# A runtime check for overfull experts moved from unit 10 to unit 3, with its transfers on POOL's queue

## The chip, the cores and the metric

The kernel runs on one core of a Trainium2 chip. A core has five engines with a queue each: TensorE (PE; its weight loads are shown apart as PEld), VectorE (DVE), ScalarE (ACT), GpSimd (POOL) and SyncE (SP), which in this kernel issues the DMA transfers. All transfers are carried by the same 16 DMA engines. The metric is the device time of one execution in microseconds (us).

## The reference

One layer of a decoder for 512 tokens of width 1024 in float32. After a mixing part (gated convolution, block-sparse attention, output projection, layer norm) comes a mixture of experts: each token picks one of 4 groups and in it 2 of 8 experts, so 2 of 32. Expert `e` computes the following on its tokens, and its result is added to the token's row with a weight:

```python
hid = jax.nn.silu(xb @ w_gate[e]) * (xb @ w_up[e])
return hid @ w_down[e]
```

A gated per-layer embedding is added, and a last layer norm closes the layer. How many tokens an expert gets is known only at run time.

## The kernel before

**Units.** The 32 experts are sorted by their number of tokens and cut into 12 units, `KINDS = "PPPQPQPQPQPP"`: a P unit holds 2 experts with 64 places each, a Q unit 4 experts with 32 places each. Unit 3 is the first Q unit, unit 4 a P unit, unit 10 the last but one. The loop over `n` runs them in order. A unit has 8 steps `gate_up` (a slice of 128 input channels each, PE rows `L1003`), a `swiglu`, and 4 steps `down` (`L1023`), for which `f` counts from 0 to 3. Between the steps PE does other work that is due (`pace`, `fill`): it gathers the tokens of later units (`L764`, `L765`), adds the results of the last unit to the tokens' rows (`scatter`, `L1035`), and works on the per-layer embedding. `drain` does what is left of it. Unit 11 has down steps of its own (`last_down`, `L1340`), and after them come the last scatters (`L1352`, `L1353`), the layer norm and the stores.

**Loads.** 24 slots of 1 MB lie in on-chip memory. Each step of a P unit needs one slot of weights and each step of a Q unit two; a slot is filled by two transfers of 512 KB that SP issues (`L266`; `L273` for the last four). `pump` hands out slots to the loads in the order of the queue for as long as more than `reserve` slots are free; `serve` calls it after each step with 0. A transfer that fills a used slot waits on SP for the last reader of the slot, and SP issues in order, so everything behind it waits too. At most eight transfers are under way. Where `queue[0][0]` stands in `closed`, the pump stops: the constants of the last norm (`("ln2",)`, issued at `L235`) are held back in this way until unit 11.

**The check.** An expert with more tokens than places needs further passes. `count_blocks` in unit 2 writes the number of these passes to `nxi`. `overflow` loads that number on each engine (`L1066`) and jumps over the body where it is zero (`L1067`); on the inputs timed here it is zero. Every engine runs this code. The arm that is taken for zero passes adds to each engine's semaphore, and to that of each transfer queue used in the body, what the body would have added. An engine or queue first waits there for its own earlier work. The body borrows the first four free slots. Before the change, `overflow` stands in unit 10, between its last `down` and the copies out of its result (`L1029`, `L1030`).

Of the kernel before, what the change touches and what calls it, by code (L numbers as in the profile page):

```python
# [18 lines left out]
P = 128  # L19
# [13 lines left out]
NU = len(KINDS)  # L33
NFIX = 4
# [17 lines left out]
PLE = {5: 5, 6: 1, 7: 4, 8: 1, 9: 5}  # L52
WEIGHTS = {"P": [1.5, 0, 1.5, 0] + [5, 2.5] + [0, 1, 0], "Q": [2, 2, 2, 1.5] + [3, 2] + [1, 2, 1]}
LAST = [4, 0, 4, 0, 2, 2]


C_ID = 0
# [7 lines left out]
C_KEY = C_MASK + P  # L65
C_KE = C_KEY + (NBLK - 1) * NE
C_KO = C_KE + (NBLK - 1) * NE
C_END = C_KO + (NBLK - 1) * NE
# [31 lines left out]
def hybrid_moe_layer_kernel(ctx: ExitStack, tc: tile.TileContext, xT, xtok, pT, w_in, w_conv, w_out, ln1, w_r,  # L100
                            b_r, w_e, w_last, w_pg, w_pp, ln2, cst, out):
    nc = tc.nc
# [5 lines left out]
    slots = Slots(upool, N_SLOTS)  # L108
    banks = {"mm": 2, "s": 3, "y": 2, "z": 1}

    def ps(tag):
        return psum.tile([P, 512], F32, tag=tag, name=f"ps_{tag}", bufs=banks[tag])

    def sm(name, shape, dtype=F32, bufs=2):
        return spool.tile(list(shape), dtype, tag=name, name=name, bufs=bufs)
# [20 lines left out]

    queue = deque()
    loaded = {}
    closed = {("ln2",), ("e", NFIX // 2, 0, 0)}

    def pump(reserve, ahead=99):
        while queue and slots.left() > reserve and len(loaded) < ahead and queue[0][0] not in closed:
            key, src, shape = queue.popleft()
            b = slots.take(shape)
            if callable(src):
                src(b.t)
            else:
                nc.sync.dma_start(b.t, src)
            loaded[key] = b

    wants, got = deque(), {}

    def claim(key, shape, dtype=F32, urgent=False):

        (wants.appendleft if urgent else wants.append)((key, shape, dtype))

    def serve(all_=True):
        while wants and slots.left():
            key, shape, dtype = wants.popleft()
            got[key] = slots.take(shape, dtype)  # L160
        if all_ and not wants:
            pump(0)

    def grab(key):
        if key not in got:
# [3 lines left out]
    def need(key):  # L169
        while key not in loaded:  # L170
            pump(slots.left() - 1)
        return loaded.pop(key)
# [76 lines left out]
    for n in sorted(PLE):  # L249
        t = sum(len(v) for v in tasks.values())  # L250
        tasks[n] = list(range(t, t + PLE[n]))
    rows_of, base = w_e.rearrange("n u p i d -> (n u p i) d"), {}
# [490 lines left out]
    def ple_start():  # L743

        for j in range(2):
            for i in range(2):
                claim((("x", j), i), [P, KD, 2 * P], F32R)
            yield (("x", j), 1)
            ple["x", j] = [grab((("x", j), i)) for i in range(2)]
            add(3.6, ple_turn(j))  # L750
            yield
# [18 lines left out]
    def ple_chunk(c):  # L770
        for i in range(2):
            claim((("pg", c), i), [P, KD, 256], F32R)
        yield (("pg", c), 1)
        yield from halve(("pg", c), need(("pg", c)))
# [244 lines left out]
    def down(o, f, ht, ws, cap):  # L1019
        for h in range(2):  # L1020
            for i, w in enumerate(ws):
                r = slice(i * cap, (i + 1) * cap)
                nc.tensor.matmul(o[h][r], ht[:, f, r], w[:, h * 512:(h + 1) * 512], start=(f == 0), stop=(f == 3))  # L1023
# [41 lines left out]
    def overflow():  # L1065
        nv = nc.values_load(nxi[0:1, 0:1], min_val=0, max_val=2 * T // CAP + NE)  # L1066
        with tc.If(nv > 0):  # L1067
            own = list(slots.q)
            ws, wb, tb, kb = own[0:4]
            kt = upool.tile([P, 4 * T], F32, tag=f"u{kb}", name="kt")  # L1070
            n = (NBLK - 1) * NE
            nc.sync.dma_start(kt[:, 0:3 * n], cst[:, C_KEY:C_END])
            kv, ke, ko, keys = (kt[:, i * n:(i + 1) * n].rearrange("p (b e) -> p b e", e=NE) for i in range(4))
            find_blocks(keys)
            nc.vector.tensor_mul(keys, keys, kv)
# [7 lines left out]
            with tc.For_i(0, nv) as _:  # L1083
# [18 lines left out]
                rv = nc.values_load(ei[0:1, 0:1], min_val=0, max_val=(NP - 1) * ROWS + 1)  # L1102
# [23 lines left out]
                def piece_of(u):  # L1126
                    t = upool.tile([P, 2, D], F32, tag=f"u{ws}", name="wo")
                    for r in range(2):
                        nc.sync.dma_start(t[:, r], rows_of[bass.ds(rv + (2 * u + r) * 2 * P, P, 2)])
                    return t  # L1130

                o = [ps("mm") for _ in range(2)]
                for u in range(4):
                    t = piece_of(u)
# [6 lines left out]
                for u in range(2):  # L1141
                    t = piece_of(4 + u)
# [10 lines left out]
    def add(cost, gen, lane=1):  # L1153
        lanes[lane].append((cost, gen))
# [22 lines left out]
    def fill(share):  # L1177

        spare[0] += share * (rest(0) + rest(1))
        while (lanes[0] or lanes[1]) and spare[0] > 0:  # L1180
            spare[0] -= any_piece()
        spare[0] = min(spare[0], 1.0)
# [7 lines left out]
    def chore():  # L1190

        while chores and (lack[0] is None or lack[0] in got):
            try:
                lack[0] = next(chores[0])
                return True
            except StopIteration:
                chores.popleft()
        return False
# [3 lines left out]
    def place_pair(n):  # L1202
        places[n] = t = sm("pt", [P, T], F32R, bufs=1)
        e, m, cap = UNITS[n]
        place(t, lambda tt: rmb[:, tt, e:e + m], m, cap)
        yield 0.3
# [13 lines left out]
    for n in range(NU):  # L1220
        g, r = GROUP_OF[n]
        ne, cap = UNITS[n][1:]
        o = [ps("mm") for _ in range(2)]
        point = [0]

        def pace():
            w = (LAST if n == NU - 1 else WEIGHTS[KINDS[n]])[point[0]:]
            if w[0]:
                fill(w[0] / sum(w))
            point[0] += 1  # L1230

        def pieces(u):
            return [need(("e", n, j, u)) for j in range(ne // 2)]

        if scat is not None:
            add(3.6, scat, 0)
        add(0.3, place_pair(n), 0)
        done[:] = [0.0, 0.0]
        ahead = n == GROUPS[g][-1] and g + 1 < NG
        if ahead:  # L1240
            claim(("xe", g + 1), [P, KD, GROUP], F32, True)
            if g % 2:
                claim(("pts", g + 1), [P, NT, 2 * GROUP], F32R, True)
        for t in tasks.get(n, []):
            add(3.5, ple_task(t))
        if n + 2 == min(tasks):
            chores.append(ple_start())
        for t in tasks.get(n + 1, []):
            if t % NT == 0:
                chores.append(ple_chunk(t // NT))  # L1250
        chore()
        for k in range(KD):
            bs = pieces(k)
            gate_up(o, k, [xe[g].t[:, k, r * P + i * cap:r * P + (i + 1) * cap] for i in range(ne)],
                    [b.t[:, i] for b in bs for i in range(2)])
            slots.give(*bs)
            if n == NU - 1 and k == 1:
                closed.clear()
                slots.q.rotate(-4)
            serve()  # L1260
            if k == 1 and ahead:
                select(g + 1)
                add(7.7 if len(GROUPS[g + 1]) > 1 else 5.3, gather_group(g + 1))
            if k > 0:
                chore()
            if n == 0 and k == 0:
                next(weights)
                next(steps)
            if n == 0 and k == 1:
                rank(mc, 0, NT, NE)  # L1270
                next(weights)
            if n == 0 and k == 4:
                late[0] = group_weights(0)
                next(late[0])
            if r == 0 and k == 6:
                for _ in late.pop(g):
                    pass
            if n == 2 and k == 6:
                count_blocks()
            if k % 2:  # L1280
                pace()
        h = sm("hw", [P, FE], bufs=1)
        swiglu(h, o, wsl[g][r], P)
        pace()
        ht = turn_hidden(h, P)
        pace()
        if n == NU - 1:
            drain()
            break
        o = [ps("y") for _ in range(2)]  # L1290
        if n == 0:
            for j in range(2):
                claim(("acc", j), [P, 2, D])
        for f in range(4):
            bs = pieces(8 + f)
            down(o, f, ht, [b.t[:, i] for b in bs for i in range(2)], cap)
            slots.give(*bs)
            if f == 3:
                claim("y", [P, 4 * T], F32R, True)
            serve()  # L1300
            chore()
            if f < 3:
                pace()
        y = grab("y")
        if n == NU - 2:
            overflow()
            serve()
        for h in range(2):
            split_out(halves(y.t, h), o[h], P)
        scat = scatter_pair(n, y.t, y)  # L1310
        while chore():
            pass
        if n == NU - 2:
            drain()
        if n == GROUPS[g][-1]:
            drain()
            slots.give(xe.pop(g))

    n, y, sq, diag = NU - 1, slots.take([P, 4 * T], F32R), slots.take([P, 512]), slots.take([P, 2, P])
    pt = places.pop(n)  # L1320
# [2 lines left out]
    u = sm("u", [P, 2, NT], bufs=1)  # L1323
# [227 lines left out]
```

## Time and profile before

| what | value |
|---|---|
| median of 3 runs | 764.24 us (761.93 to 764.78) |
| the profiled execution | 761.77 us, of it 760.0 us span from the first to the last instruction |
| PE busy | 727.2 us, 96% of the span |
| DMA | 233.52 MB, 307 GB/s over the span |
| mean granted TensorE clock | 0.994 of full speed |

The span is shown in the profile in 40 slices of 19 us. Times "at 704.3" below are us from the span's start. An engine's idle time is put down to what ended it; a busy PE is not PE at its peak, since matmuls overlap and their ends are modelled.

### The profile page before, as it was taken

The numbers are of one execution on the slowest core, as the hardware profiler recorded it, in microseconds if no ns is written. First come the engines' busy times: TensorE is split into PE (matmuls) and PEld (weight loads), VectorE is DVE, ScalarE is ACT, GpSimd is POOL, SyncE is SP. The second block draws the span as 40 slices with busy tenths as digits, with TensorE's granted clock in tenths as the row PEclk, the third lists the DMA queues.
The fourth block names the chain that finished last, engine by engine and source line by source line (L and its number), as shares of the span: only waits on it lengthen the run. The fifth ranks groups of instructions, "written<-read, shape, count | busy, mean of one in ns | idle before, by whom it ended". The sixth has DMA issues, their size and how long they took to land. (4 is left out here: it accounts for less than half of the span.)

```text
span 760.0 us, 11561 instructions
## 1 busy us (share of the span) xinstructions
PE 727.2 (96%) x4338; PEld 431.2 (57%) x4338; DVE 312.5 (41%) x657; ACT 163.9 (22%) x340; POOL 66.5 (9%) x93
## 2 busy tenths in 40 slices
PE   7999999999999899999989999999999999999896
PEld 4787887787878336335723437444465444653243
DVE  4656544647588426251525103332023321223246
ACT  5445544243021101010312001200012000110015
POOL 0215335100000000000000000000000000100002
PEclk9999999999999999999999999999999999999999
DMA  8500401355509999999999999999999999999972
GB/s 297 225 1 1 166 1 35 132 229 223 213 5 374 421 411 362 376 410 409 406 410 408 391 401 356 374 408 409 403 406 394 409 410 408 409 407 410 407 261 111
DMA packets 61979, 233.52 MB, mean 307 GB/s; under 512 B 6864, under 2 KB 10592, under 8 KB 56032
## 3 DMA queue, kind: packets, MB, share of 16 engines
q1 hardware_dynamic: 61920, 232.75, 78.2%
q8 instruction: 35, 0.57, 0.3%
q14 instruction: 24, 0.20, 0.1%
HBM read 230.62 MB, written 2.10 MB: 306 GB/s over the span
## 5 line engine op out<-in xcount | busy, mean ns | idle before, releaser
L1003 PE MATMUL ps_mm<-big,big 128*64 128x512 f32 (+1 forms) x1024 | 217.1, 603 | 12.8 <-DMA big<-in_w_e_dram 9.4
L1003 PEld LDWEIGHTS ps_mm<-big,big 128*64 128x64 f32 (+1 forms) x1024 | 56.2, 123 | 148.4 <-issue 87.9
L1044 DVE TENSOR_TENSOR big<-big,ps_s 128x512 f32<-128x512 f32 x80 | 52.0, 683 | 129.3 <-PE ps_s L1035 129.3
L132 PE MATMUL ps_mm<-big,big 128*128 128x512 f32 (+1 forms) x240 | 89.9, 375 | 3.4 <-ACT big L118 3.4
L133 PE MATMUL ps_mm<-big,big 128*128 128x512 f32 (+1 forms) x240 | 87.1, 363 | 0.2 <-DVE big L119 0.2
L134 PE MATMUL ps_mm<-big,big 128*128 128x512 f32 (+1 forms) x240 | 86.9, 362 | 0.1
L1023 PE MATMUL ps_y<-big,ht 128*32 128x512 f32 (+1 forms) x480 | 82.9, 604 | 0.7 <-ACT ht L1016 0.7
L119 DVE TENSOR_TENSOR big<-big,big 128x512 fp32r<-128x512 f32 (+1 forms) x74 | 58.5, 823 | 27.5 <-ACT big L118 26.9
L118 ACT CAST big<-big 128x512 fp32r<-128x512 f32 (+1 forms) x74 | 50.6, 727 | 43.3 <-DVE big L433 20.1
L1035 PE MATMUL ps_s<-big,pt 128*128 128x512 f32 x176 | 57.9, 433 | 0.7 <-DVE big L1044 0.6
L132 PEld LDWEIGHTS ps_mm<-big,big 128*128 128x128 f32 x240 | 45.3, 189 | 14.3 <-ACT big L118 4.8
L134 PEld LDWEIGHTS ps_mm<-big,big 128*128 128x128 f32 x240 | 45.3, 189 | 7.8 <-DVE big L119 0.6
L133 PEld LDWEIGHTS ps_mm<-big,big 128*128 128x128 f32 x240 | 45.3, 189 | 6.7 <-DVE big L119 0.8
L1035 PEld LDWEIGHTS ps_s<-big,pt 128*128 128x128 f32 x176 | 28.5, 189 | 32.6 <-issue 24.7
L807 POOL TENSOR_TENSOR big<-big,ps 128x256 f32<-128x256 f32 x16 | 11.8, 735 | 400.6 <-issue 178.1
L375 POOL TENSOR_SCALAR big<-big,rden 128x128 f32<-128x128 f32 (+3 forms) x32 | 39.1, 1232 | 70.5 <-DVE rden L373 70.5
L1023 PEld LDWEIGHTS ps_y<-big,ht 128*32 128x32 f32 (+1 forms) x480 | 22.0, 124 | 40.7 <-issue 37.1
L813 PEld LDWEIGHTS ps_s<-big,big 128*128 128x128 f32 x320 | 41.4, 190 | 5.9 <-issue 3.3
L813 PE MATMUL ps_s<-big,big 128*128 128x256 f32 x320 | 43.8, 285 | 0.1
L132 PE MATMUL ps_s<-big,big 128*128 128x256 f32 x128 | 37.0, 289 | 0.1
L134 PE MATMUL ps_s<-big,big 128*128 128x256 f32 x128 | 36.2, 283 | 0.0
L133 PE MATMUL ps_s<-big,big 128*128 128x256 f32 x128 | 36.2, 283 | 0.0
(263 smaller groups left out, 765.0 us busy)
## 6 DMA issues: line engine op xcount, KB each, us to landing
big<-in_w_e_dram SPq DMA_DIRECT2D x336, 512.0 KB, 10.1
big<-in_w_e_dram SPq DMA_DIRECT2D x24, 1024.0 KB, 15.2
big<-in_w_in_dram SPq DMA_DIRECT2D x11, 1024.0 KB, 6.4
big<-in_w_out_dram SPq DMA_DIRECT2D x4, 1024.0 KB, 5.9
big<-in_w_pg_dram SPq DMA_DIRECT2D x4, 1024.0 KB, 9.3
big<-in_xtok_dram SPq DMA_DIRECT2D x2, 1024.0 KB, 6.9
out_dram<-big SPq DMA_DIRECT2D x8, 256.0 KB, 2.0
big<-in_xT_dram SPq DMA_DIRECT2D x3, 512.0 KB, 8.5
```

The lines of the kernel that those rows point to most:

```text
L118: nc.scalar.copy(hi, raw)
L119: nc.vector.tensor_sub(lo, raw, hi.bitcast(F32))
L132: nc.tensor.matmul(o, ah, bh, start=first, stop=False)
L133: nc.tensor.matmul(o, ah, bl, start=False, stop=False)
L134: nc.tensor.matmul(o, al, bh, start=False, stop=last)
L375: nc.gpsimd.tensor_scalar(pr[h][:, 0:ks], pr[h][:, 0:ks], rden[:, h:h + 1], None, op0=ALU.mult)
L807: nc.gpsimd.tensor_tensor(r, r, s, op=ALU.add)
L813: nc.tensor.matmul(o[:, 0:n], src[tt // 2].t[:, tt % 2, k * P:(k + 1) * P], pt(tt), start=(i == 0), stop=(i == 2 * NT - 1))
L1003: nc.tensor.matmul(o[a][i * m:(i + 1) * m], x, w[:, a * FE:(a + 1) * FE], start=(k == 0), stop=(k == KD - 1))
L1023: nc.tensor.matmul(o[h][r], ht[:, f, r], w[:, h * 512:(h + 1) * 512], start=(f == 0), stop=(f == 3))
L1035: nc.tensor.matmul(o, pt[0:m, tt * P:(tt + 1) * P], y[i][0:m], start=(i == 0), stop=(i == 1))
L1044: nc.vector.tensor_add(r, r, o)
```

## The change

The check is made at the end of unit 3 (`CHECK = 3`), after the unit's result is copied out and all work due is drained. For the last two down steps of that unit the pump keeps four slots back (`kept[0] = 4`) and gives them out after the check. The transfers inside the body are issued by POOL (`nc.gpsimd`) in place of SP. The constants of the last norm are no longer held back, and the four slots at the end are no longer set apart (`slots.q.rotate(-4)` goes).

```diff
+CHECK = 3
-    closed = {("ln2",), ("e", NFIX // 2, 0, 0)}
+    closed = {("e", NFIX // 2, 0, 0)}
-    wants, got = deque(), {}
+    wants, got, kept = deque(), {}, [0]
...
         if all_ and not wants:
-            pump(0)
+            pump(kept[0])
...
-            nc.sync.dma_start(kt[:, 0:3 * n], cst[:, C_KEY:C_END])
+            nc.gpsimd.dma_start(kt[:, 0:3 * n], cst[:, C_KEY:C_END])
...
-                        nc.sync.dma_start(t[:, r], rows_of[bass.ds(rv + (2 * u + r) * 2 * P, P, 2)])
+                        nc.gpsimd.dma_start(t[:, r], rows_of[bass.ds(rv + (2 * u + r) * 2 * P, P, 2)])
...
-            if n == NU - 1 and k == 1:
-                closed.clear()
-                slots.q.rotate(-4)
...
             bs = pieces(8 + f)
+            kept[0] = 4 if n == CHECK and f > 1 else 0
...
-        if n == NU - 2:
-            overflow()
-            serve()
...
         if n == GROUPS[g][-1]:
             drain()
             slots.give(xe.pop(g))
+        if n == CHECK:
+            overflow()
+            kept[0] = 0
+            serve()
```

The following rows are PE's before the change at the end of unit 10. `big300` and `big301` hold the weights of its last two down steps, and `nxi` the number of further passes; `L1083` is the loop in the body.

```order
L1023 MATMUL ps_y_5763<-big300_5563,ht_5753 64x512 x2
L1023 MATMUL ps_y_5764<-big300_5563,ht_5753 64x512 x2
L1023 MATMUL ps_y_5763<-big301_5566,ht_5753 64x512 x2
L1023 MATMUL ps_y_5764<-big301_5566,ht_5753 64x512 x2
L1066 TENSOR_LOAD nxi_2312
L1067 COMPARE_AND_BRANCH
L1083 COMPARE_AND_BRANCH
L1083 UNCONDITIONAL_BRANCH x2
```

After the change these two steps of unit 10 are followed by unit 11's first `gate_up`. The next rows are PE's after the change at the end of unit 3, with line numbers that are higher by one. `big157` and `big158` are the weights of unit 3's last down step.

```order
L766 MATMUL ps_s_3371<-marks_3197,big90_2043 128x128
L1024 MATMUL ps_y_3258<-big157_3133,ht_3226 32x512 x2
L1024 MATMUL ps_y_3258<-big158_3136,ht_3226 32x512 x2
L1024 MATMUL ps_y_3259<-big157_3133,ht_3226 32x512 x2
L1024 MATMUL ps_y_3259<-big158_3136,ht_3226 32x512 x2
L1067 TENSOR_LOAD nxi_2312
L1068 COMPARE_AND_BRANCH
L1084 COMPARE_AND_BRANCH
L1084 UNCONDITIONAL_BRANCH x2
```

In the kernel before, the same four rows of unit 3 are followed by unit 4's first `gate_up`. The body between the jump and its target is 112 such rows on PE, in both kernels. The last rows are SP's after the change at the same place: `big164` is the third piece of unit 4's weights, `big166` the fourth.

```order
L267 DMA big164_3315<-in_w_e_dram 128x1024
L267 ISA
L267 DMA big164_3315<-in_w_e_dram 128x1024
L1067 TENSOR_LOAD nxi_2312
L1067 ISA x2
L1068 COMPARE_AND_BRANCH
L1084 COMPARE_AND_BRANCH
...
L1068 UNCONDITIONAL_BRANCH
L267 ISA
L267 DMA big166_3667<-in_w_e_dram 128x1024
```

Before the change SP goes on from the third piece to the fourth with nothing between. The fourth piece, and with it every later load, now stands behind the check and waits for PE to have passed it, since the slot is one of those that the body might have used.

## Rows read from the trace of the kernel before

**Rows 1.** The page: GB/s of the transfers in 40 slices of the span.

```profile
GB/s 297 225 1 1 166 1 35 132 229 223 213 5 374 421 411 362 376 410 409 406 410 408 391 401 356 374 408 409 403 406 394 409 410 408 409 407 410 407 261 111
```

**Rows 2.** What SP waited for: us in total, times, longest.

```profile
SPq L266 <- DMA big<-in_w_e_dram: 145.2, 193, 2.0
SPq L266 <- PE ps_mm L1003: 55.5, 33, 4.7
```

**Rows 3.** What PE waited for from 404 to 700 us.

```profile
PE ps_mm L1003 <- DMA big<-in_w_e_dram: 6.9, 27, 0.6
```

**Rows 4.** The check's two lines: op, duration ns min/median/max, first and last start.

```profile
L1066 PEldq TENSOR_LOAD <-nxi x1: 491/491/491, 703.7 to 703.7; - x1
...
L1067 SPq EVENT_SEMAPHORE  x9: 17/17/17, 728.2 to 735.9; - x9
...
L1067 PEldq COMPARE_BRANCH  x1: 6092/6092/6092, 704.3 to 704.3; - x1
L1067 DVEq COMPARE_BRANCH  x1: 72/72/72, 704.7 to 704.7; - x1
L1067 SPq COMPARE_BRANCH  x1: 53/53/53, 727.7 to 727.7; - x1
```

**Rows 5.** PE in order of time around the check: start, us, what [idle before].

```profile
703.82 3.60 PE L1023 MATMUL ps_y<-big,ht 128*64 128x512 f32 x16
710.88 5.18 PE L1003 MATMUL ps_mm<-big,big 128*64 128x512 f32 x16 [3.46 <-PEq L1067]
...
717.59 7.09 PE L1003 MATMUL ps_mm<-big,big 128*64 128x512 f32 x32
```

**Rows 6.** The stretch after it: length, busy PE, PEld, DVE, ACT, POOL, PEclk, DMA share, GB/s.

```profile
710.80:714.30 3.50, 3.42 (x10) 1.25 (x12) 0.00 (x0) 0.00 (x0) 0.00 (x0) 0.54 1.03 410
```

**Rows 7.** The chain that ended last: start, us, what; its first pieces and the last downs.

```profile
710.88 5.18 PE ps_mm L1003 x16
...
732.76 5.30 PE ps_y L1340 x32
...
739.19 1.01 PE ps_mm L1340 x8
```

**Rows 8.** Stretches in which the last weights arrive, columns as in rows 6.

```profile
734.50:735.00 0.50, 0.50 (x6) 0.21 (x4) 0.00 (x0) 0.00 (x0) 0.00 (x0) 1.00 0.07 23
735.00:735.50 0.50, 0.50 (x6) 0.16 (x4) 0.00 (x0) 0.00 (x0) 0.00 (x0) 1.00 0.00 0
```

**Rows 9.** PE at the end of unit 3 and the start of unit 4.

```profile
379.26 1.92 PE L1023 MATMUL ps_y<-big,ht 128*32 128x512 f32 x16
382.85 0.64 PE L1003 MATMUL ps_mm<-big,big 128*64 128x512 f32 x1 [1.67 <-DMA big<-in_w_e_dram]
```

**Rows 10.** PE's groups in unit 4's gate_up: busy us, mean ns, idle before.

```profile
L1003 PE MATMUL ps_mm<-big,big 128*64 128x512 f32 x64 | 18.9, 608 | 2.5 <-DMA big<-in_w_e_dram 2.5
L1035 PE MATMUL ps_s<-big,pt 128*128 128x512 f32 x5 | 2.0, 459 | 0.0
```

**Rows 11.** SP's issue of the fourth piece of unit 4, and the transfers' times to landing.

```profile
379.16 0.33 SPq L266 DMA_DIRECT2D big<-in_w_e_dram  x1
...
big<-in_w_e_dram SPq DMA_DIRECT2D x336, 512.0 KB, 10.1
...
big<-in_w_pg_dram SPq DMA_DIRECT2D x4, 1024.0 KB, 9.3
```

**Rows 12.** Transfers while unit 4 starts, and after two long waits of SP.

```profile
380.00:390.00 10.00, 7.91 (x34) 2.15 (x28) 2.65 (x5) 2.96 (x4) 0.00 (x0) 1.00 1.02 408
301.00:305.00 4.00, 4.00 (x23) 1.92 (x23) 1.77 (x4) 0.37 (x1) 0.00 (x0) 1.00 0.83 273
470.00:474.00 4.00, 4.00 (x36) 1.69 (x32) 0.30 (x1) 0.37 (x1) 0.00 (x0) 1.00 0.79 293
474.00:478.00 4.00, 4.00 (x34) 3.28 (x26) 1.11 (x2) 0.37 (x1) 0.00 (x0) 1.00 0.81 255
```

**Rows 13.** The page: the queue that brings code: packets, MB, share.

```profile
q8 instruction: 35, 0.57, 0.3%
```

## The prediction

> **What bounds the kernel now.** I read the GB/s line of the page first. From some 240 to 727 us the transfers run at 350 to 420 GB/s, mostly 405 to 410 [rows 1], which is as fast as they go anywhere. The waits of SP agree: it waits 145.2 us for earlier transfers to land and 55.5 us for `gate_up` to free a slot [rows 2]. So the stream of weights paces the experts, and TensorE follows it closely. After 404 us it waits for weights 27 times, 6.9 us in all and 0.6 us at most [rows 3]. A stop of TensorE can therefore be made good there, while a stop of the stream cannot.
>
> Then I read the check's two lines. TensorE needs 0.49 us to load the number and 6.09 us for its jump, the DVE and SP jumps 0.07 and 0.05 us [rows 4]. TensorE's order of time shows what of it costs: its sequencer gets to the check at 703.7, ahead of 16 matmuls that start at 703.82 and end at 707.42, and the next matmul starts at 710.88, after 3.46 us without work [rows 4, 5]. [...] Its first 16 matmuls take 5.18 us, while 32 take 7.09 us a little later, so 16 take 3.55 [rows 5]. The clock costs another 1.6 us, and the check 5.1 us of TensorE.
>
> Is that on the path that sets the end? The chain that ended last goes from 710.88 on through TensorE alone, up to the last weights' first use at 739.19 [rows 7]. The weights are there before: the last bytes move between 734.5 and 735.0 [rows 8], and SP, which waits in the check for all its transfers, goes on at 735.9 [rows 4]. I take 735.5 for their landing. So TensorE is 3.7 us behind the last weights, and the 5.1 us are what put it there.
>
> **What the change removes.** Without the check in unit 10, TensorE would come 5.1 us earlier to every step of unit 11. It cannot use the last weights before they land, so the end comes earlier by the smaller number, **3.6 us** (a tenth is left for the start), with bounds of 3.3 (landing at 735.9) and 4.2 (at 735.0). SP's wait from 728.2 to 735.9 [rows 4] goes too, and the norm's constants land earlier. They are not in the chain, so I cost this at nothing.
>
> **What the change adds at the end of unit 3.** Six parts.
>
> TensorE's stop. Unit 3's last 16 matmuls run from 379.26 to 381.18, and the next matmul waits for weights until 382.85, so 1.67 us are idle now [rows 9]. If the sequencer again comes to the check as its last 16 matmuls start, about 379.2, and the jump takes 6.09 us again, the next matmul starts 7.2 us later (710.88 less 703.7), at 386.4: 3.5 us late. The lower clock adds 1.6 us, as before. If the jump is as short as the other engines' (0.05 to 0.07 us), nothing is lost, since the idle 1.67 us cover it.
>
> What makes the 5.1 us good. In unit 4's `gate_up`, from 382.85 to 404.1, 64 matmuls `L1003` would take 14.2 us at the rate of 32 in 7.09 [rows 5], the scatters take 2.0 [rows 10]; the rest of 21.2 us is 5.0 us of slack. It holds the late start almost to a tenth, and the 6.9 us of waits after 404 [rows 3] hold a remainder. So this stop costs nothing by itself. Without that cover it would cost up to 5.1 us.
>
> The four slots. SP now issues the fourth piece of unit 4 at 379.16 [rows 11]. After the change this transfer, and all behind it in SP's queue, wait until TensorE is through the overflow check: some 381.3 with a short jump (the end of its last matmuls), some 386.1 with a long one (379.2 + 0.49 + 6.09, and 0.3 for what lies between). What is then under way? By the order of SP's queue the six transfers of 512 KB of unit 4's first three pieces, and ahead of them a piece of the embedding's weights of 1 MB, which takes 9.3 us to land [rows 11]. That is 4 MB, or about 10.2 us at 408 GB/s [rows 12]; the median of 10.1 us from issue to landing says the same [rows 11]. So the stream lasts until about 389.4, and SP comes back 8 or 3.3 us ahead of that. With 8 us nothing is lost. For 3.3 us the nearest rows are the two places at which SP came back from its longest waits for TensorE: around 301 the stream fell to 273 GB/s for 4 us, a loss of 1.3 us against 408, and from 470 to 478 to 293 and 255, a loss of 2.6 us [rows 12]. The stream should fall only where nothing is left under way, and here 3.3 us of it are. I take **0.3 us**, near to nothing, with bounds of 0 and 2.6.
>
> SP's own part of the check (its jump at 727.7 and the first wait behind it at 728.2, so some 0.5 us [rows 4]) lies in its wait for the slots. It no longer waits for its own transfers, since the body uses none of SP's.
>
> POOL's part. Its lanes are unused, so its arm waits for none of them. `nxi` is ready since unit 2, and POOL's next work in the program, an addition for the embedding, is due only in unit 5. SP waits for POOL's arm, which is passed long before.
>
> ACT and DVE come to the check after copying out unit 3's result. With jumps like DVE's of 0.07 us [rows 4] they lose little, and in unit 4 TensorE waits for neither before its first scatter.
>
> **Sum.** 3.6 less 0.3 makes 3.3 us. The profiled execution took 761.77 us, so the same execution would take 758.5 us. It lies 2.5 us under the median of the runs shown and just under the fastest, 761.93. Set against the median of 764.24, the forecast is **760.9 us**, which is 0.43% less. About 0.5%, or 3.8 us, is what a measurement here can tell from no change.
>
> **The rivals.**
>
> A short jump. At 704.3 the jump took 6.09 us on TensorE alone, and TensorE alone jumps over 112 rows, on the other engines it is about 55 or fewer. If its price depends on where the code lies, it may be short in unit 3. Then TensorE passes at 381.3, the stream has 8 us left, and the gain is the whole 3.6 us: 760.6 us. For it speaks that code comes in 35 pieces of about 16 KB [rows 13]. [...]
>
> The stream runs dry. The jump is long and the restart costs what it did around 301 or 470, 1.3 to 2.6 us; the gain is 1.0 to 2.3 us, 762 to 763.2 us. For it: a long wait of SP on TensorE did that twice. Against it: 3.3 us are still under way here.
>
> Nothing is covered (the other side). Many transfers are held by TensorE's slots [rows 2]. If its lateness goes on into the stream, the whole 7.2 us of the jump and 1.6 us of the clock are lost in unit 4: 8.8 less 3.6 is 5.2 us more, 769.4 us. It decides from 7.4 us lost in unit 3 on. Against it stand 1.67 us of idle time, 4 MB under way and the slack.
>
> No gain at the end. If the last weights were later needed for other reasons, or landed 3 us later by small delays of the stream, the time would stay, about 764 us.
>
> **Chances.** Forecast 0.30, short jump 0.37, dry stream 0.20, nothing covered 0.06, no gain 0.07. The first two, at 760.9 and 760.6, lie just short of the bound of 0.5% (760.4), and the runs themselves spread by 0.37%. Of their 0.67 I give 0.38 to faster by over 0.5% and 0.29 to within it; the dry stream and no gain are within, 0.27. That makes faster 0.38, same 0.56, slower 0.06. For the range: 764.24 less the upper bound of 4.2 and less half of the spread of the runs gives 758.6; at the top it takes in the dry stream with its bound and part of no gain, 764.0.
>
> **What would show it.** In the trace after: no idle TensorE at the end of unit 10 and the full clock there. Waits for weights in unit 11, with the last use of weights within 0.1 us of their landing, near 735.5. At the end of unit 3 a jump on TensorE of 6.09 or of under 0.1 us, which tells the first two cases apart. GB/s at 380 to 400 near 408, or a dip below 300 for some us (dry stream). If TensorE waits less than 5 us in unit 4 and after, the slack is wrong; if it still trails the weights at the end, the sum is.

## The result, and the profile after

| | before | changed | ratio, 95% interval |
|---|---|---|---|
| first series, median of 4 and 4 runs | 763.28 us | 756.27 us | 0.9915 (0.9887 to 0.9944) |
| second series, median of 23 and 6 runs | 761.0 us | 757.17 us | 0.9940 (0.9916 to 0.9963) |
| the profiled execution | 761.77 us, span 760.0 | 755.91 us, span 754.2 | |

The changed kernel is faster, by 0.85% in the first series and by 0.60% in the second, which ran on another occasion with both kernels unchanged. The ratios are not the quotients of the medians, which are 0.9908 and 0.9950. The forecast was 0.43% and 760.9 us; its range ended at 758.6, and both series lie below it. In the experiments further below, one run of the kernel before took 1136.0 us at a mean granted clock of 0.556, and no ratio counts it.

The page of the changed kernel, GB/s in 40 slices of 18.9 us (compare [rows 1]), and what SP waited for in the whole span (us in total, times, longest; compare [rows 2]):

```profile
GB/s 304 222 1 1 168 1 27 133 225 216 238 1 381 421 413 348 366 407 408 407 407 409 401 399 377 364 408 408 409 406 402 408 409 408 409 407 410 408 334 111
```

```profile
SPq L267 <- DMA big<-in_w_e_dram: 138.4, 187, 1.9
...
SPq L267 <- PE ps_mm L1004: 56.6, 31, 4.7
...
SPq L267 <- PEq L1068: 2.2, 1, 2.2
...
SPq L267 <- DVEq L1068: 0.8, 1, 0.8
```

The stream still paces the experts. The new waits are the last two lines: the first transfer after the check waits 2.2 us for TensorE, and the third, issued at 382.53, waits 0.8 us for VectorE. The check's two lines, now at the end of unit 3 (compare [rows 4]):

```profile
L1067 PEldq TENSOR_LOAD <-nxi x1: 489/489/489, 378.5 to 378.5; - x1
...
L1068 DVEq EVENT_SEMAPHORE  x2: 21/21/21, 382.3 to 382.4; - x2
...
L1068 SPq EVENT_SEMAPHORE  x1: 17/17/17, 376.9 to 376.9; - x1
L1068 PEldq COMPARE_BRANCH  x1: 445/445/445, 379.1 to 379.1; - x1
...
L1068 DVEq COMPARE_BRANCH  x1: 72/72/72, 381.7 to 381.7; - x1
```

TensorE's jump takes 0.445 us, not 6.09. SP has one event in its arm at 376.9 where it had nine from 728.2 to 735.9. TensorE in order of time at the end of unit 3 (compare [rows 9]) and where the check was, in unit 10 (compare [rows 5]):

```profile
378.47 1.92 PE L1024 MATMUL ps_y<-big,ht 128*32 128x512 f32 x16
382.37 3.27 PE L1004 MATMUL ps_mm<-big,big 128*64 128x512 f32 x10 [1.98 <-DVEq L1068]
...
701.67 3.61 PE L1024 MATMUL ps_y<-big,ht 128*64 128x512 f32 x16
705.10 3.60 PE L1004 MATMUL ps_mm<-big,big 128*64 128x512 f32 x16
```

TensorE is idle 1.98 us at the new place, where it was idle 1.67 before anyway, and the matmul that ends this starts at 382.37, against 382.85. It waits for VectorE now, which copies out the unit's result before it comes to the check (its jump is at 381.7). By the trace's record of each transfer the weights landed at 381.99, so this part of the check holds TensorE for 0.4 us. At the old place nothing is idle any more, and the first 16 matmuls of unit 11 take 3.60 us in place of 5.18. The stretches around these (length, busy PE, PEld, DVE, ACT, POOL, granted clock, DMA share, GB/s; compare [rows 12] and [rows 6]):

```profile
380.00:390.00 10.00, 7.83 (x30) 2.31 (x27) 2.92 (x4) 2.84 (x4) 0.00 (x0) 1.00 1.02 405
...
705.00:708.50 3.50, 3.50 (x18) 1.01 (x14) 1.38 (x2) 0.66 (x2) 0.00 (x0) 1.00 1.02 405
```

The stream does not dip at the new check, and the clock is full at the old one. The chain that ended last (compare [rows 7]), and the last weights' first use in TensorE's order of time:

```profile
706.16 10.92 DMA big<-in_w_e_dram
717.12 1.93 PE ps_mm L1004 x6
...
727.12 5.46 PE ps_y L1340 x32
```

```profile
733.64 1.08 PE L1340 MATMUL ps_mm<-big,ht 128*64 128x256 f32 x8
```

The chain now runs through the stream up to 717.12 and only then through the work of unit 11; before, it ran through that work from 710.88 on. By the trace's record of each transfer the last weights land at 733.4 and are used at 733.64. TensorE trailed them by 3.6 us before and does so by 0.2 now. So of the 5.86 us between the two profiled executions, 3.4 are TensorE's trailing, 2.1 are a stream that ends earlier (735.5 to 733.4), and the remaining 0.4 lie elsewhere, mostly behind the last weights.

### The profile page after: what moved, and what is told of

It is laid out like the page before. It is cut to its first block, busy times and chain, and to the rows that moved or that the text cites. A ratio compares the mean times of both kernels' runs of the same rounds, so it can differ in the third digit from the quotient of the medians.

```text
span 754.2 us, 11580 instructions
## 1 busy us (share of the span) xinstructions
PE 726.4 (96%) x4338; PEld 433.5 (57%) x4338; DVE 312.5 (41%) x657; ACT 164.3 (22%) x340; POOL 66.6 (9%) x93
## 5 line engine op out<-in xcount | busy, mean ns | idle before, releaser
L1024 PE MATMUL ps_y<-big,ht 128*32 128x512 f32 (+1 forms) x480 | 81.2, 597 | 0.7 <-ACT ht L1017 0.7
```

## The experiments

Ten runs followed, two of them of the kernels before and after unchanged. Two questions were open: why the jump was short, and whether the stream's 2.1 us belong to the change. My theory: the position of TensorE's code decides the jump, the change's gain is the long jump gone from unit 10, and the 2.1 us are scatter. The rivals: the moment or the length of the jump decides, or the change also feeds the stream better. Each series has its own runs of the kernel before; a result gives the median, that of the kernel before, and the ratio.

The changed kernel again is the second series above. Expected were 757.3 to 758.5 us if only TensorE's trailing is gained, and 756.3 within 0.4 if the stream gains too. Its 757.17 lies 0.1 under the first and above the second.

**The kernel before again.** No edit.

> The kernel before, unchanged, for a second trace and for the scatter of its times. Of the 5.86 us between the two profiled executions, 3.4 us are TensorE no longer trailing the last weights, and 2.1 us are a stream of weights that ends earlier (733.4 in place of 735.5). Theory A, the 2.1 us are scatter of single executions (0.7 us of it is there before 12 us already): this trace's stream ends up to 2 us away from 735.5 and its jump takes 6.1 us again, give or take 0.3. Theory B, the 2.1 us come from the change: the stream ends at 735.5 within 0.4 us. Theory C, the jump's price varies from run to run: it is away from 6.09 us by more than 1 us, and the time with it.

Measured 761.17 us (759.31 to 765.06 in 12 runs) against 761.65, 1.0005 (0.9988 to 1.0023). In the trace the jump, and SP's events in its arm, of which the last follows the landing of the last weights (735.9 in [rows 4]):

```profile
L1067 SPq EVENT_SEMAPHORE  x9: 17/17/17, 725.8 to 733.2; - x9
L1067 PEldq COMPARE_BRANCH  x1: 6032/6032/6032, 701.8 to 701.8; - x1
```

The stream ends 2.7 us earlier in another execution of the very same kernel, earlier than in the changed one, and the jump is the same to 0.06 us. So B and C fall, and A holds, though the stream's end moved by more than its 2 us. The stream's end is what scatters: by the trace's record of each transfer, over the nine traces in which nothing holds it long at unit 3 its last weights land from 732.6 to 735.9.

**No check at all.** From the kernel before; further passes are left out.

```diff
         if n == NU - 2:
-            overflow()
             serve()
```

> The kernel before without the overflow check; the further passes of an overfull expert are left out. If the check at the end of unit 3 costs nothing, this kernel takes the time of the changed one, 756.3 us within 0.6. If the check in its new place costs what I forecast as the price of a held stream, this kernel is 0.3 to 2.6 us faster than the changed one, 753.7 to 756.0. If the changed kernel gained by something else than by clearing unit 10 (POOL's queue, the constants of the norm let go earlier), this kernel stays behind it by over 1 us, at 757.3 or more.

Measured 758.24 us against 761.65, 0.9947 (0.9928 to 0.9966). By its number this is the third case: 758.24 is over 1 us behind the 756.3 of the first series. But the changed kernel's second series has 757.2, and by the ratios, 0.9947 and 0.9940, the two lie 0.5 us apart and their intervals overlap widely. So these runs show neither a price of the check at its new place nor a gain beside the clearing of unit 10; some 2 us of either would not show.

**A shorter body, check left in unit 10.** Five eighths of the gather in the body are left out; no engine enters the body here.

```diff
-                for k in range(KD):
+                for k in range(3):
                     gather_piece(xo, lambda tt: se[:, tt], k, CAP)
```

> The kernel before with the check where it was, in unit 10, and a shorter body that no engine enters here: of the body's gather 3 of 8 slices are left (5 are left out), so that TensorE jumps over some 230 instructions and not 310. Theory A, the jump is long because its target lies in code that TensorE does not hold, and the distance decides: the jump takes under 0.6 us as in unit 3 of the changed kernel (0.445 us), no stretch at half clock follows, and the time falls by 3.4 to 5 us to 758.3 to 760 us (SP still waits for its own transfers before the norm's constants). Theory B, it is long because of when it is made (late, with the stream full): 6.1 us again, and 763.3 us within 0.6.

Measured 757.71 us against 761.65, 0.9951 (0.9934 to 0.9968). The jump, and TensorE in order of time behind it:

```profile
L1067 PEldq COMPARE_BRANCH  x1: 353/353/353, 703.0 to 703.0; - x1
```

```profile
702.45 3.60 PE L1023 MATMUL ps_y<-big,ht 128*64 128x512 f32 x16
706.51 3.77 PE L1003 MATMUL ps_mm<-big,big 128*64 128x512 f32 x16 [0.46 <-PEq L1067]
```

Code that is never executed was 4.4 us of TensorE's time: the idle time falls from 3.46 to 0.46 us, and the 16 matmuls behind it from 5.18 to 3.77. The place in unit 10 is not dear; the jump was. So A holds for the jump, and the time is 0.6 us under its lower end.

In this trace SP's wait, which stays in unit 10, comes onto the path. SP's events, and TensorE's first matmul with the norm's constants:

```profile
L1067 SPq EVENT_SEMAPHORE  x9: 17/17/17, 726.8 to 734.5; - x9
```

```profile
741.49 1.99 PE L1413 MATMUL ps_mm<-big,cs 128*128 128x512 f32 x4 [1.07 <-DMA big<-in_ln_dram]
```

The constants are issued after the last of these events, and TensorE is idle for 1.07 us until they land.

**The same code, moved by 118 instructions, check left in unit 10.** The body is whole. If the position of the code decides, the jump's duration may change; if its length or its unit does, it takes 6.0 to 6.1 us again.

```diff
     for _ in range(WARM):
         nc.tensor.matmul(warm, zerob, onesb[:, 0:1].to_broadcast([P, 512]), start=True, stop=True)
+    for _ in range(59):
+        nc.tensor.matmul(warm[:, 0:16], zerob, onesb[:, 0:16], start=True, stop=True)
```

> The kernel before, with 59 more matmuls of 16 columns in its warm-up loop at the very start, which move all of TensorE's later code by 118 instructions; check, body and the length of its jump (310 instructions) are those of the kernel before. [...]

Measured 758.06 us against 762.72, 0.9951 (0.9932 to 0.9969). The jump in the trace, SP's events, and TensorE behind the jump:

```profile
L1069 SPq EVENT_SEMAPHORE  x9: 17/17/17, 726.0 to 732.9; - x9
...
L1069 PEldq COMPARE_BRANCH  x1: 353/353/353, 702.1 to 702.1; - x1
```

```profile
705.65 3.65 PE L1005 MATMUL ps_mm<-big,big 128*64 128x512 f32 x16 [0.46 <-PEq L1069]
```

The position decides, and neither the length nor the unit: the same jump over the same 310 instructions at the same point of the program costs 0.35 us in place of 6.03 to 6.09. Fifty-nine more matmuls at the start, 1.7 us of work, make the kernel 0.5% faster. Here SP's last event is at 732.9, and TensorE does not wait for the norm's constants.

**The changed kernel, code moved by 138 instructions.** The same edit with 69 matmuls, for the same question about the short jump of 0.445 us.

> The changed kernel, with 69 more matmuls of 16 columns in its warm-up loop at the very start, which move TensorE's later code by 138 instructions; the check, the four slots and the jump's length (315 instructions) are unchanged. [...]

Measured 758.65 us against 762.72, 0.9953 (0.9937 to 0.9969). The jump, and the stretch from 384 to 396 us:

```profile
L1070 PEldq COMPARE_BRANCH  x1: 6152/6152/6152, 377.4 to 377.4; - x1
```

```profile
384.00:396.00 12.00, 12.00 (x44) 3.95 (x44) 2.96 (x3) 1.99 (x2) 0.00 (x0) 0.88 0.99 336
```

The long jump is back, now in unit 3, and with it a dip of the stream: 336 in place of 407 GB/s over 12 us, 72 short of 408, so 2.1 us lost. By the ratios the time is 1.0 us over the changed kernel's, but its interval reaches that kernel's 0.9940: the jump and the dip show the loss, the time alone doesn't.

The traces' records of the code queue [rows 13] suggest what TensorE waits for in a long jump: its code. In all six traces with one, a 16 KB packet of code begins 3.5 to 3.6 us into the jump, takes 1.1 us, and the jump ends 1.4 us after it. In the five traces with a short jump none falls into it.

**The changed kernel with a longer body.** No engine enters it here.

```diff
-                for k in range(KD):
+                for k in 3 * list(range(KD)):
                     gather_piece(xo, lambda tt: se[:, tt], k, CAP)
```

> The changed kernel, check at the end of unit 3, with a longer body that no engine enters here: its gather stands three times, so that TensorE jumps over some 570 instructions in place of 315. Theory A, distance decides the jump, and what follows covers it (the case that I forecast): the jump takes 6 us or more, TensorE starts unit 4 some 3.5 us late and at half clock for 3.5 us, its waits for weights from 383 to 500 shrink by 5 us, the stream dips for some us around 385, and the time is 756.3 us plus 0 to 0.8. Theory B, nothing is covered: 3.5 to 9 us slower, 760 to 765. Theory C, distance does not decide: jump 0.4 us, 756.3.

Measured 759.36 us against 761.65, 0.9966 (0.9949 to 0.9983). The jump, TensorE behind it, and the stream:

```profile
L1068 PEldq COMPARE_BRANCH  x1: 6083/6083/6083, 379.2 to 379.2; - x1
```

```profile
385.75 5.26 PE L1004 MATMUL ps_mm<-big,big 128*64 128x512 f32 x16 [5.25 <-PEq L1068]
```

```profile
384.00:386.00 2.00, 0.24 (x2) 0.28 (x4) 0.00 (x0) 0.00 (x0) 0.00 (x0) 0.91 0.95 373
386.00:388.00 2.00, 2.00 (x6) 0.57 (x6) 0.00 (x0) 0.00 (x0) 0.00 (x0) 0.50 0.95 332
...
384.00:396.00 12.00, 10.24 (x39) 3.63 (x41) 2.96 (x3) 1.99 (x2) 0.00 (x0) 0.86 0.96 329
```

This is the case that I had forecast for the change: TensorE goes on at 385.75 (forecast 386.4), and its first 16 matmuls take 5.26 us. But the stream loses (408 less 329) x 12 / 408 = 2.3 us, and neither theory has the price: it is above A's 0.8 and below B's 3.5, 2.0 us over the changed kernel by their ratios of 0.9966 and 0.9940 (whose intervals overlap). That is about the size of the dip.

**The long body, with one piece of weights let past the check.** From the kernel with the long body:

```diff
-            kept[0] = 4 if n == CHECK and f > 1 else 0
+            kept[0] = 6 if n == CHECK and f > 1 else 0
...
             overflow()
+            slots.q.rotate(-4)
             kept[0] = 0
```

> The changed kernel with the body that TensorE jumps over in 6 us (its gather stands three times), and with the four slots that the body borrows put behind the other free slots once the check is written, so that the fourth piece of unit 4 (two transfers, 1 MB, 2.6 us of stream) need not wait for TensorE; the fifth and later ones still do. With the long jump alone the stream fell to 199 to 373 GB/s from 384 to 396 us, 2.3 us lost, and the time was 759.36. Theory A, that loss came from SP being held by TensorE with too little under way: with 1 MB more under way the dip is gone or under 0.7 us in sum, TensorE's late start at 385.8 is made good by its slack, and the time is 757.2 to 758.2. Theory B, TensorE's lateness itself reaches the stream through the slots that it frees late: the dip stays at 2 us or more and the time at 759.4 within 0.5.

Measured 757.03 us against 761.0, 0.9946 (0.9925 to 0.9967). Jump and stream, and what TensorE waited for from 376 to 400 us:

```profile
L1068 PEldq COMPARE_BRANCH  x1: 6023/6023/6023, 379.4 to 379.4; - x1
```

```profile
384.00:396.00 12.00, 10.07 (x36) 3.39 (x38) 2.96 (x3) 1.99 (x2) 0.00 (x0) 0.74 1.02 407
```

```profile
PE ps_mm L1004 <- PEq L1068: 5.2, 1, 5.2
```

TensorE stops for as long as before and runs at 0.74 of its clock over these 12 us, yet the stream holds 407 GB/s, TensorE waits for no weights until 400, and the last weights are again used 0.1 us after they land. A holds: what the long jump cost was the stream that SP could not feed, and TensorE's own lateness is made good. The time is 0.2 us under A's span and that of the changed kernel within the scatter.

**POOL's queue alone, check in unit 10.** From the kernel before; the same edit for the second transfer of the body.

```diff
-            nc.sync.dma_start(kt[:, 0:3 * n], cst[:, C_KEY:C_END])
+            nc.gpsimd.dma_start(kt[:, 0:3 * n], cst[:, C_KEY:C_END])
```

> The kernel before with the check where it was, in unit 10, but the body's transfers on POOL's queue. SP then no longer waits there for its own transfers (728.2 to 735.9 before). The norm's constants are still held until unit 11. TensorE's jump stays 6.0 to 6.1 us. Theory A, SP's wait is off the path that sets the end: 761.7 us within 0.6. Theory B, SP's wait or the late constants are part of the gain: over 1 us faster.

Measured 761.79 us against 761.0, 1.0011 (0.9996 to 1.0026). SP's arm and the jump:

```profile
L1067 SPq EVENT_SEMAPHORE  x1: 17/17/17, 726.9 to 726.9; - x1
...
L1067 PEldq COMPARE_BRANCH  x1: 6052/6052/6052, 703.8 to 703.8; - x1
```

SP's nine events are one, its wait of 7.7 us is gone, and the time is the same. A holds: behind the long jump that wait was off the path.

**The changed kernel, body's transfers on SP's queue.** The reverse edit, at the end of unit 3.

> The changed kernel with the check at the end of unit 3, but the body's transfers on SP's queue as before. In the arm for zero passes SP now waits for all that it has under way, which by the order of landings lasts until some 388.5 us, before it issues the fourth piece of unit 4. Theory A, POOL's queue is what makes the place affordable: the stream runs dry for the 2 us and more that a first transfer needs from issue to landing, and comes back slowly; 2.5 to 5 us lost, 760 to 763 us. Theory B, the loss is covered as a long jump's partly was: within 1 us of the changed kernel.

In the traces of the profiled pair the shortest median from issue to landing is 2.0 us, of the stores of 256 KB; the shortest of a load is 3.7 us, of 256 KB in the changed kernel.

Measured 763.1 us against 761.0, 1.0031 (1.0011 to 1.0051). SP's arm and two stretches of the stream:

```profile
L1068 SPq EVENT_SEMAPHORE  x9: 17/17/17, 377.6 to 390.0; - x9
```

```profile
384.00:396.00 12.00, 9.04 (x28) 2.31 (x30) 2.96 (x3) 1.99 (x2) 0.00 (x0) 0.99 0.64 229
...
396.00:400.00 4.00, 4.00 (x8) 0.74 (x4) 0.00 (x0) 0.00 (x0) 0.00 (x0) 0.60 0.95 246
```

SP waits until 390.0 for all that it has under way, and the stream loses 5.3 and 1.6 us in these two stretches, 6.9 in all. The kernel is 5.9 us slower than the changed one of the same series, slower than before the change, and 0.1 us above the upper end of A's span of 760 to 763. In the place in unit 3 the queue is worth nearly all of this; in unit 10, with the long jump, it was worth nothing.

## Why the prediction missed, point by point

**What bounds the kernel, and the 3.6 us: right.** TensorE's trailing behind the last weights went from 3.6 to 0.2 us in the profiled pair. In the 5.1 us that the prediction counts for the check are 1.6 of a lower granted clock, 0.54 in [rows 6]; behind a short jump in unit 10, or none there, the same 16 matmuls took 3.60 to 3.77 us. The kernel without a check and the two with a short jump in unit 10 gained 3.7 to 4.0 us by their ratios.

**TensorE's stop in unit 3: the wrong case.** The forecast took the jump as 6.09 us again. It took 0.445, so the rival with a short jump held, and by the cause that it named: padding made the old jump short and the new one long, over unchanged distances. The jumps over 310 and 315 instructions cost 0.35 to 0.45 us in one position and 6.0 to 6.2 in the other, and one over 570 cost 6.0 to 6.1. The prediction itself gave this rival 0.37 and its forecast 0.30. Which positions are dear, the runs do not tell: of the four in which these jumps over 310 and 315 instructions lay, two were. The traces have a packet of code inside each long jump and inside no short one, and put the price at some 5.7 us (6.02 to 6.15 less 0.35 to 0.45).

**The four slots: the mechanism right, the case and the size wrong.** With the short jump they cost nothing (405 GB/s from 380 to 390). For the long jump I took 0.3 us, since the stream should fall "only where nothing is left under way". It fell from 384 to 386 us already, to 373 GB/s, while the transfers ahead of the check still had until 388.7 to land; the loss was 2.1 to 2.3 us, near the upper bound of 2.6. The rows around 301 and 470 were the better measure, and the rival of the dry stream, with its 1.3 to 2.6 us, had the right price for this case. Had the jump been long, the gain would have been 2.6 us by the long body's ratio, 761.6 us on the prediction's base. That the sum of 3.3 us came near the 3.6 of the short jump is luck: the low price stood for a case that would have cost some 2 us.

**TensorE's slack: right.** With the stream kept full, 5.2 us of stop and a lower clock cost nothing at the end that the runs can tell.

**ACT and DVE: a wait overlooked.** The prediction says that TensorE waits for neither in unit 4 before its first scatter. The first matmul of unit 4 waits for DVE's part of the check, for 0.4 us longer than for its weights, and SP waits for it for 0.8 us; the slack and the transfers under way cover both.

**POOL's queue and SP's wait: right for this change.** Behind the long jump SP's wait in unit 10 was off the path, and in unit 3 SP's own queue would have cost 5.9 us. But "not in the chain" was read with the long jump in place. With a short jump and SP's wait still in unit 10, the norm's constants came late by 1.07 us in one of two traces.

**The number and its range: here is the miss.** The mechanisms sum to 3.6 us, close to the forecast's 3.3, and the second series, 0.9940 (0.9916 to 0.9963), is 4.6 us (3.8 by the medians) with an interval that holds both. The step that failed is the last one, "764.24 less the upper bound of 4.2 and less half of the spread of the runs gives 758.6". It took a median of three runs as the base and half of their spread, 1.4 us, as all that a single series could add. The kernel before has a median of 761.0 to 762.7 in the longer series, with single runs from 756.6 to 765.1; the ends of its stream alone scatter by 2.6 us between two traces. The 4 runs of the changed kernel came out at 755.9 to 756.6, the same kernel's later 6 at 754.3 to 757.6. Set against these medians, 3.6 us less is 757.4 to 759.1; the second series and the three kernels above lie at 757.2 to 758.2. Measured by the second series, the first one's 7.0 us are 3.8 of gain, 2.3 of a base that lay high, and 0.9 of four runs of the changed kernel that lay low. As a share of the time before, the range went from 0.74% less to nearly nothing, and the 0.60% of the second series lies inside it. The profiled execution of before was 2.5 us under its median; the prediction noted that and still hung the sum on the median.

What remains open: why the stream ends up to 3.3 us earlier or later in these executions, 2.6 in two of one kernel. By the records of the transfers the same weights land 0.4 us apart in the profiled pair at 426 us and 2.0 apart at 499. That stretch lies behind the check in unit 3, but the second trace of the kernel before gains 1.2 us there on the first one too.

## What to carry to other kernels

A conditional jump that is always taken can cost 6 us on one engine by where its code happens to lie (on TensorE here 6.0 to 6.2 us, or 0.35 to 0.45), so read the jump's own duration in the trace, and where it is long, shorten or shift the skipped code before moving the check. What may be late at such a place is the engine that has slack (here 5.2 us of TensorE's stop, with the stream kept full, cost nothing that the runs can tell), not the queue that feeds a saturated stream (SP's, held in unit 3, cost 5.9 us): let its next transfers depend on nothing in the skipped part, slots and queue alike. Take the base and the width of a forecast from many runs: here the median of three lay 1.5 to 3.2 us above those of the longer series, nearly as much as the effect.

## What the hardware showed that I had not expected

Code that is never run, and 59 tiny matmuls ahead of everything, each moved the end by 3.7 us, by the ratios. The stream loses rate while several transfers are still under way: in the trace of the long body SP was held until 385.4, three of the earlier transfers were still under way at 386, the last of them until 388.7, and the stream was at 332 GB/s from 386 to 388. And the clock falls to half without any jump: in the trace with POOL's queue and the check in unit 10, TensorE waited 2.21 us for weights ahead of unit 4 and was then granted 0.50 of its clock, while in the changed kernel it was idle for 1.98 us at the same place and kept 1.00:

```profile
383.44 6.01 PE L1003 MATMUL ps_mm<-big,big 128*64 128x512 f32 x16 [2.21 <-DMA big<-in_w_e_dram]
```

```profile
384.00:386.00 2.00, 2.00 (x5) 0.75 (x5) 0.00 (x0) 0.23 (x1) 0.00 (x0) 0.50 1.02 408
```
